# A hybrid attention and state-space layer on one core: x in whole tiles without GpSimd, y's second half in two groups, the last products and stores spread over more engines

## The chip, the cores and the metric

The kernel runs on one core of one Trainium2 chip. The metric is the time of one execution in microseconds (us); less is better. TensorE (PE) multiplies matrices, VectorE (DVE) and ScalarE (ACT) work element by element, GpSimd (POOL) does so too, and SyncE (SP) issues the transfers between HBM and the on-chip memory.

## The reference, cut to what matters

```python
hn = rms_norm(x, norm_mix)
q, k, v, gate_a, u, gate_s = split(hn @ w_in)          # 2048 -> 4608 columns
y_attn = block_attention(rope(rms(q)), rope(rms(k)), v) * silu(gate_a)
y_ssm = gelu(s5_bidirectional(u))
glu = y_ssm @ w_glu + b_glu
y_ssm = glu[:, :1024] * sigmoid(glu[:, 1024:]) * silu(gate_s)
h = x + concat(y_attn, y_ssm) @ w_out
h = h + sigmoid(rms_norm(h, norm_ple) @ w_ple_gate) * (p @ w_ple_proj)
return rms_norm(h, norm_final)                          # (1, 1024, 2048)
```

There are 1024 tokens and 2048 features, all in float32. Features lie on the 128 partitions and tokens along the free side, so x is 16 tiles (k = 0 to 15) of 128 features by 1024 tokens.

## The kernel before

Each matrix product is made of three: an operand is split into a rounded part H (ScalarE: a copy, for x with the gain as scale) and the rest L = operand minus H (VectorE), and TensorE forms H·H, H·L and L·H. Weights come in tiles of 512 columns (wraw, three buffers), and their H and L (wH, wL) have four buffers each; `w_next` hands out one tile, starts the load of the tile four further on and the split of the tile two further on.

The program is written in one order, and each engine takes its own instructions in that order; semaphores make an instruction wait for its operands and for the buffers that it overwrites. SyncE's queue is in order too: a load that waits for its buffer holds up every transfer behind it. Side work runs as generators (`bg`), each of which takes one step at each `tick`, two k tiles apart.

**The first stage** (`run`, the loop over k): for every k tile, `mm_k` forms the products with two columns of w_in (tile zf, 12 matmuls of 512 tokens per k). Around it `x_dma(k + 4)` loads x, `x_split(k + 2)` makes hH (L310, ScalarE) and hL (L311, VectorE), and `x_sq(k + 1)` sums the squares for the norm: the left token half is squared (L493) and added (L495) on GpSimd, the right half squared on ScalarE (L491) and added on VectorE (L495). Weight tiles change at every fourth k. The third column of w_in (zt) follows without a gap in the program, then the other columns with the state-space scan beside them, then attention.

**The back part** (`back(hf)`) runs once for each token half hf: products with w_glu, w_out, and then 16 rounds n of 48 matmuls with w_gate and 6 with w_proj; `fin_g` closes a round with a sigmoid (ScalarE, L1133) and a square (L1149). In the first half, the second half's y is fetched after round 10 (`y_load`, eight loads into the ring of nine buffers `cyc`), passed through GELU after round 11 (L1064, eight on ScalarE), and split in the background (`y_split`). ScalarE loads another table (ACT_TABLE_LOAD) whenever it changes between sigmoid and GELU.

**The end** (`finish(1)`): `colsum` sums the squares over the partitions with eight one-column matmuls, alternately of the running sum `acc` and of the last tile's squares; `rsqrt` and `spread` follow on VectorE, `rows` (L360) spreads the result over all partitions into PSUM, ScalarE copies it to `acc` (L1166), and VectorE forms 16 products (L1169), each stored by SyncE (L1170).

Of the kernel before, what the change touches and what calls it, by code (L numbers as in the profile page):

```python
# [9 lines left out]
F32 = mybir.dt.float32  # L10
F32R = mybir.dt.float32r
I32 = mybir.dt.int32
ALU = mybir.AluOpType
# [3 lines left out]
SEQ = 1024  # L17
# [221 lines left out]
class Kernel:  # L239
# [63 lines left out]
    def split(self, H, L, src, scale=None):  # L303

        nc = self.nc
        if scale is None:
            nc.scalar.copy(H, src)  # L307
            nc.vector.tensor_tensor(L, src, H.bitcast(F32), ALU.subtract)  # L308
        else:
            nc.scalar.activation(H, src, AF.Copy, scale=scale)  # L310
            nc.vector.scalar_tensor_tensor(L, src, scale, H.bitcast(F32), ALU.mult, ALU.subtract)  # L311
# [21 lines left out]
        nc.vector.tensor_scalar(t, t, -0.5, 1.5, ALU.mult, ALU.add)  # L333
        nc.vector.tensor_tensor(out, r, t, ALU.mult)

    def colsum(self, sqs, more=None):


        pc = self.psC("cs")
        for i, sq in enumerate(sqs):  # L340
            for b in range(4):
                c, s = 4 * i + b, slice(128 * b, 128 * b + 128)
                self.nc.tensor.matmul(
                    pc[:, c : c + 1], sq[:, s], self.ones[:, 0:1], start=True, stop=more is None
                )
                if more is not None:
                    self.nc.tensor.matmul(pc[:, c : c + 1], more[i][:, s], self.ones[:, 0:1], start=False, stop=True)
        return pc[:, 0 : 4 * len(sqs)]

    def spread(self, cols):  # L350
# [112 lines left out]
    def x_dma(self, k):  # L463
        if k >= KD:
            return
        for h in range(2):
            xt = self.xp.tile([128, 512], F32, name="xraw", tag="xraw", bufs=10)
            self.nc.sync.dma_start(xt, self.i["xT"][k][:, self.half(h)])
            self.xraw.append(xt)

    def x_split(self, k):
        H = self.b4(f"hH{k}", dt=F32R)
        L = self.b4(f"hL{k}", dt=F32R)
        self.hH.append(H)
        self.hL.append(L)
        for h in range(2):
            s = self.half(h)
            self.split(H[:, s], L[:, s], self.xraw[2 * k + h], self.g_mix[:, k : k + 1])

    def x_sq(self, k):  # L480
        nc = self.nc
        for h in range(2):
            s = self.half(h)
            xt = self.xraw[2 * k + h]
            self.xraw[2 * k + h] = None
            if k == 0:
                nc.scalar.activation(self.xsq[:, s], xt, AF.Square)
                continue
            sq = self.xp.tile([128, 512], F32, name="xq", tag="xq", bufs=4)
            if h:  # L490
                nc.scalar.activation(sq, xt, AF.Square)  # L491
            else:
                nc.gpsimd.tensor_tensor(sq, xt, xt, ALU.mult)  # L493
            eng = nc.vector if h else nc.gpsimd
            eng.tensor_tensor(self.xsq[:, s], self.xsq[:, s], sq, ALU.add)  # L495

    def x_rstd(self):
        self.rstd = self.xsq
# [549 lines left out]
            if k % 2:  # L1048
                self.tick()

    def y_load(self, hf):
        raw = []
        for j in range(8):
            t = self.cyc()
            self.nc.sync.dma_start(
                t.rearrange("p (t c) -> p t c", t=4),
                self.d_y[j][4 - 4 * hf : 8 - 4 * hf].rearrange("t f c -> f t c"),
            )
            raw.append(t)
        return raw  # L1060
# [7 lines left out]
            yield  # L1068
        self.y_gelu(raw)

    def y_split(self, hf, raw, yg, pool=False):
        split = self.split_pool if pool else self.split
        for j in range(8):
            x = self.hl(f"yg{hf}_{j}")
            v = x.rearrange("p r (t c) -> p r t c", t=4)
            split(v[:, 0], v[:, 1], raw[j].rearrange("p (t c) -> p t c", t=4)[:, ::-1, :])
            yg[j] = x
            yield

    def o_load(self, hf, mix, js=range(8)):  # L1080
        for j in js:
# [46 lines left out]
    def fin_g(self, hf, n, pg, pp, ho, hp):  # L1128
        nc = self.nc
        acc = self.xsq[:, 512:1024]  # L1130
        t = self.t2k("tz")
        nc.vector.tensor_tensor(t, pg, self.xsq[:, 0:512], ALU.mult)
        nc.scalar.activation(t, t, AF.Sigmoid)  # L1133
        last = hf == 1 and n == 15
        if last:
            nc.scalar.activation(self.rk[:, 0:1], self.ones[:, 0:1], AF.Sqrt)
        nc.vector.tensor_tensor(t, pp, t, ALU.mult)
        eng = nc.vector if last else nc.gpsimd
        eng.tensor_tensor(hp, ho, t, ALU.add)
        if last:  # L1140
            self.last_sq = self.t2k("tq")
            nc.scalar.activation(self.last_sq, hp, AF.Square)
            return
        yield
        if n == 0:
            nc.scalar.activation(acc, hp, AF.Square)
        else:
            s2 = self.t2k("tq")
            nc.scalar.activation(s2, hp, AF.Square)  # L1149
            nc.gpsimd.tensor_tensor(acc, acc, s2, ALU.add)  # L1150

    def finish(self, hf, hs):
        nc = self.nc
        acc = self.xsq[:, 512:1024]
        if hf == 0:
            for _ in range(5):
                yield
        pc = self.colsum([acc], [self.last_sq] if hf == 1 else None)
        yield
        yield  # L1160
        self.rsqrt(pc, DM, self.rk[:, 0:4])
        dg = self.spread(self.rk[:, 0:4])
        for _ in range(5):
            yield
        r = self.rows(dg)
        nc.scalar.copy(acc, r)  # L1166
        for n in range(16):
            g = self.g_fin[:, n : n + 1]
            nc.vector.scalar_tensor_tensor(hs[n], hs[n], g, acc, ALU.mult, ALU.mult)  # L1169
            nc.sync.dma_start(self.out[n][:, self.half(hf)], hs[n])  # L1170
            if hf == 0:
                yield

    def p_load(self, hf, pT):
        for k in range(2):
# [7 lines left out]
    def back(self, hf, yg, mix):  # L1183
# [19 lines left out]
        for n in range(16):  # L1203
            if n % 2 == 0:
                hp = self.b4(f"h{hf}_{n}", (128, 2, 512))
            pg = self.psC("pg")
            ho = self.cyc()
            nc.sync.dma_start(ho, self.d_h[hf][n])
            if n == 0:
                self.bg(self.h_rstd())  # L1210
            self.mm_half(pg, 16, hg)
            pp = self.psC("pp")
            self.mm_half(pp, 2, pT)
            hs.append(hp[:, n % 2])
            self.bg(self.fin_g(hf, n, pg, pp, ho, hs[n]))
            if hf == 0 and n == 10:
                raw = self.y_load(1)
            if hf == 0 and n == 11:
                self.y_gelu(raw)
                self.bg(self.y_split(1, raw, nyg))  # L1220
        self.drain()
        self.bg(self.finish(hf, hs))
        return nyg, nmix
# [11 lines left out]
    def run(self):  # L1235
# [62 lines left out]
        yg, mix = {}, {}  # L1298
        for b in self.attention():
            if b == T * (NH - 1) + 2:  # L1300
                self.bg(self.y_split(0, raw, yg, True))
            elif b == NH * T + 3:
                self.bg(self.o_load(0, mix))
        for hf in range(2):
# [101 lines left out]
```

## Time and profile before

| | us |
|---|---|
| median of three runs (2195.22 to 2196.39) | 2195.66 |
| the profiled execution's own time | 2196.16 |
| its span | 2194.4 |
| TensorE busy in the span | 2129.4 |
| VectorE, ScalarE, GpSimd busy | 1384.1, 780.0, 656.0 |

The profiled execution is 1.76 us longer than its span, and 0.50 us above the median of the runs. The profile's slices (40 of 54.9 us) show TensorE at 7 tenths in the first, 6 tenths in the last and 9 or more in all between; VectorE is at 8 tenths in the first slice, GpSimd at 6. A timeline row gives the start, the length, the engine, the line, what is written and read, and in brackets how long the engine had been idle and who ended that. Matmuls overlap, so their pitch is read from their starts.

### The profile page before, as it was taken

What the parts mean: (1) busy time and instruction counts of PE and PEld (TensorE: products, weight loads), DVE (VectorE), ACT (ScalarE), POOL (GpSimd) and SP (SyncE); (2) the same over time, 40 slices, a digit from 0 to 9 for tenths busy, and PEclk for the clock granted to TensorE, in tenths of its full rate; (3) what the DMA queues carried; (4) which work ended last, traced back from release to release, by engine and by line L of the source; (5) the groups of instructions that cost most, each with busy time, mean ns of one, the idle gap of its engine ahead of it and who ended that gap; (6) DMA issues with size and microseconds to landing.
All of it is one profiled execution on the core that took longest, in us unless ns stands there. A gap on an engine that the chain in (4) does not pass through costs nothing.

```text
span 2194.4 us, 29198 instructions
## 1 busy us (share of the span) xinstructions
PE 2129.4 (97%) x10428; PEld 1777.3 (81%) x10428; DVE 1384.1 (63%) x2292; ACT 780.0 (36%) x1438; POOL 656.0 (30%) x630
## 2 busy tenths in 40 slices
PE   7999999999999999999999999999999999999996
PEld 5788878888887888887889888888887788888885
DVE  8745678787878787847999744444444644444344
ACT  5211222222222222237777633333334333333332
POOL 6152455555655554601222100111122000111120
PEclk8999999999999999999999999999999999999998
DMA  5224223323323333342121244444343644453333
GB/s 193 85 99 124 65 76 90 94 87 85 105 81 97 87 93 86 97 150 75 39 77 39 92 137 137 146 151 124 124 139 119 213 142 144 144 153 114 126 113 125
DMA packets 173313, 245.08 MB, mean 112 GB/s; under 512 B 27376, under 2 KB 77680, under 8 KB 172912
## 3 DMA queue, kind: packets, MB, share of 16 engines
q1 hardware_dynamic: 173168, 243.22, 35.6%
q8 instruction: 82, 1.34, 0.2%
q14 instruction: 63, 0.52, 0.1%
HBM read 189.35 MB, written 48.56 MB: 108 GB/s over the span
## 4 chain that ended last, share of the span: by engine, by line
PE 49%; DVE 3%; ACT 1%; DMA 1%; issue 1%; POOL 0%; DVEq 0%; SPq 0%; ACTq 0%
PE ph L1046 5%; PE ph L1047 5%; PE ph L1045 5%; PE pg L1047 5%; PE pg L1046 5%; PE pg L1045 5%; PE ptr L955 2%; PE pv L969 1%; PE pv L968 1%; PE pv L970 1%; PE S L925 1%; PE S L928 1%; PE S L924 1%; PE gg L1047 1%; PE gv L1047 1%; PE gv L1046 1%
## 5 line engine op out<-in xcount | busy, mean ns | idle before, releaser
L308 DVE TENSOR_TENSOR wL<-wraw,wH 128x512 fp32r<-128x512 f32 (+1 forms) x496 | 408.5, 844 | 451.1 <-ACT wH L307 449.5
L307 ACT CAST wH<-wraw 128x512 fp32r<-128x512 f32 (+1 forms) x496 | 294.0, 604 | 461.1 <-PE ph L1046 124.1
L1045 PE MATMUL pg<-hg,wH 128*128 128x512 f32 x512 | 200.8, 392 | 1.6 <-ACT wH L307 1.6
L1047 PE MATMUL pg<-hg,wL 128*128 128x512 f32 x512 | 199.9, 390 | 0.7 <-DVE wL L308 0.7
L1046 PE MATMUL pg<-hg,wH 128*128 128x512 f32 x512 | 199.7, 390 | 0.0
L1113 POOL TENSOR_TENSOR xsq<-xsq,tz 128x512 f32<-128x512 f32 x30 | 39.0, 1301 | 517.8 <-ACT tz L1112 517.8
L837 ACT COPY ks<-kp 16x224 f32<-16x224 f32 x32 | 10.8, 336 | 340.3 <-DVE ks L836 189.2
L1045 PEld LDWEIGHTS pg<-hg,wH 128*128 128x128 f32 x512 | 96.3, 188 | 22.4 <-ACT wH L307 2.0
L1047 PEld LDWEIGHTS pg<-hg,wL 128*128 128x128 f32 x512 | 96.4, 188 | 21.1 <-DVE wL L308 1.2
L1046 PEld LDWEIGHTS pg<-hg,wH 128*128 128x128 f32 x512 | 96.4, 188 | 20.5 <-issue 0.5
L519 PE MATMUL zga<-hH,wH 128*128 128x512 f32 x256 | 104.0, 406 | 0.0
L519 PE MATMUL zq<-hH,wH 128*128 128x512 f32 x256 | 103.5, 404 | 0.0
L519 PE MATMUL zgs<-hH,wH 128*128 128x512 f32 x256 | 102.6, 401 | 0.0
L520 PE MATMUL zq<-hL,wH 128*128 128x512 f32 x256 | 100.7, 394 | 0.0
L520 PE MATMUL zgs<-hL,wH 128*128 128x512 f32 x256 | 100.4, 392 | 0.0
L520 PE MATMUL zga<-hL,wH 128*128 128x512 f32 x256 | 100.2, 391 | 0.0
L1045 PE MATMUL ph<-ma,wH 128*128 128x512 f32 x256 | 99.6, 389 | 0.0
L1046 PE MATMUL ph<-ma,wH 128*128 128x512 f32 x256 | 99.6, 389 | 0.0
L1047 PE MATMUL ph<-ma,wL 128*128 128x512 f32 x256 | 99.6, 389 | 0.0
L1045 PE MATMUL ph<-ms,wH 128*128 128x512 f32 x256 | 99.6, 389 | 0.0
L1046 PE MATMUL ph<-ms,wH 128*128 128x512 f32 x256 | 99.6, 389 | 0.0
L1047 PE MATMUL ph<-ms,wL 128*128 128x512 f32 x256 | 99.6, 389 | 0.0
(420 smaller groups left out, 5432.6 us busy)
## 6 DMA issues: line engine op xcount, KB each, us to landing
wraw<-in_w_in_dram SPq DMA_DIRECT2D x144, 256.0 KB
wraw<-in_w_out_dram SPq DMA_DIRECT2D x128, 256.0 KB
wraw<-in_w_gate_dram SPq DMA_DIRECT2D x128, 256.0 KB
wraw<-in_w_glu_dram SPq DMA_DIRECT2D x64, 256.0 KB
xraw<-in_xT_dram SPq DMA_DIRECT2D x32, 256.0 KB
out_dram<-h SPq DMA_DIRECT2D x32, 256.0 KB
t<-zz SPq DMA_DIRECT2D x40, 128.0 KB
d_u<-tz SPq DMA_DIRECT2D x16, 256.0 KB
```

The lines of the kernel that those rows point to most:

```text
L307: nc.scalar.copy(H, src)
L308: nc.vector.tensor_tensor(L, src, H.bitcast(F32), ALU.subtract)
L519: nc.tensor.matmul(ps[h], H[:, kk, :], rH[:, s], start=(k == 0), stop=False)
L520: nc.tensor.matmul(ps[h], H[:, kk, :], rL[:, s], start=False, stop=False)
L924: nc.tensor.matmul(S[:, s], qH[:, qs], kH[:, s], start=True, stop=False)
L925: nc.tensor.matmul(S[:, s], qH[:, qs], kL[:, s], start=False, stop=False)
L928: nc.tensor.matmul(S[:, s], qL[:, qs], kH[:, s], start=False, stop=True)
L955: nc.tensor.transpose(pc[:, b], P[:, 512 * hf + 128 * b : 512 * hf + 128 * b + 128], self.ident)
L1045: nc.tensor.matmul(ps, H[:, k % 4], x[:, 0], start=(k == 0), stop=False)
L1046: nc.tensor.matmul(ps, H[:, k % 4], x[:, 1], start=False, stop=False)
L1047: nc.tensor.matmul(ps, L[:, k % 4], x[:, 0], start=False, stop=(k == nk - 1))
L1113: nc.gpsimd.tensor_tensor(acc, acc, s2, ALU.add)
```

## The change

x comes in tiles of 128 by 1024 (five buffers instead of ten halves), split and squared in one instruction each (k = 0 still in halves for load and split); GpSimd has no part in it. The second half of y is loaded one tile at a time between the weight loads, after round 10, in two groups of four, each with its own GELU and split (`y_next`). At the end, the sum of `acc` is formed by itself and kept in `part`, and the last tile's sum is added to it; every third h tile is scaled by its gain beforehand on ScalarE, and its product formed on GpSimd from the copy; VectorE's 11 products read the spread row from PSUM; and odd tiles are stored from ScalarE's queue.

```diff
 def colsum(self, sqs):
...
-        for h in range(2):
-            xt = self.xp.tile([128, 512], F32, name="xraw", tag="xraw", bufs=10)
-            self.nc.sync.dma_start(xt, self.i["xT"][k][:, self.half(h)])
-            self.xraw.append(xt)
+        xt = self.xp.tile([128, SEQ], F32, name="xraw", tag="xraw", bufs=5)
+        for s in [self.half(0), self.half(1)] if k == 0 else [slice(0, SEQ)]:
+            self.nc.sync.dma_start(xt[:, s], self.i["xT"][k][:, s])
+        self.xraw.append(xt)
...
+        for s in [self.half(0), self.half(1)] if k == 0 else [slice(0, SEQ)]:
+            self.split(H[:, s], L[:, s], self.xraw[k][:, s], self.g_mix[:, k : k + 1])
...
-            sq = self.xp.tile([128, 512], F32, name="xq", tag="xq", bufs=4)
-            if h:
-                nc.scalar.activation(sq, xt, AF.Square)
-            else:
-                nc.gpsimd.tensor_tensor(sq, xt, xt, ALU.mult)
-            eng = nc.vector if h else nc.gpsimd
-            eng.tensor_tensor(self.xsq[:, s], self.xsq[:, s], sq, ALU.add)
+        sq = self.xp.tile([128, SEQ], F32, name="xq", tag="xq", bufs=2)
+        nc.scalar.activation(sq, xt, AF.Square)
+        nc.vector.tensor_tensor(self.xsq, self.xsq, sq, ALU.add)
...
+    def y_next(self, yg):
+        for q in range(2):
+            raw = []
+            for j in range(4 * q, 4 * q + 4):
+                raw += self.y_load(1, [j])
+                yield
+                yield
+            yield
+            yield
+            self.y_gelu(raw)
+            yield from self.y_split(1, raw, yg, 4 * q)
...
+        if hf == 1 and n % 3 == 2:
+            nc.scalar.activation(hp, hp, AF.Copy, scale=self.g_fin[:, n : n + 1])
...
-        pc = self.colsum([acc], [self.last_sq] if hf == 1 else None)
+        pc = self.colsum([acc])
+        if hf == 1:
+            part = self.t2k("tq", (128, 4))
+            nc.vector.tensor_scalar(part, pc, 1.0, None, ALU.mult)
+            pc = self.colsum([self.last_sq])
+            nc.vector.tensor_tensor(part, pc, part, ALU.add)
+            pc = part
...
-            nc.vector.scalar_tensor_tensor(hs[n], hs[n], g, acc, ALU.mult, ALU.mult)
-            nc.sync.dma_start(self.out[n][:, self.half(hf)], hs[n])
+            if hf == 1 and n % 3 == 2:
+                nc.gpsimd.tensor_tensor(hs[n], hs[n], acc, ALU.mult)
+            else:
+                nc.vector.scalar_tensor_tensor(hs[n], hs[n], g, r if hf == 1 else acc, ALU.mult, ALU.mult)
             if hf == 0:
                 yield
+            eng = nc.scalar if hf == 1 and n % 2 else nc.sync
+            eng.dma_start(self.out[n][:, self.half(hf)], hs[n])
...
             if hf == 0 and n == 10:
-                raw = self.y_load(1)
-            if hf == 0 and n == 11:
-                self.y_gelu(raw)
-                self.bg(self.y_split(1, raw, nyg))
+                self.bg(self.y_next(nyg))
```

The order on VectorE at the start of the first stage, before (hL, wL, xsq as above; a row gives line, operation, what is written and read, the size):

```order
L308 TENSOR_TENSOR wL<-wraw,wH 128x512
L311 SCALAR_TENSOR_TENSOR hL_220<-xraw,vec,hH_219 128x512 x2
L308 TENSOR_TENSOR wL<-wraw,wH 128x512 x2
L311 SCALAR_TENSOR_TENSOR hL_260<-xraw,vec,hH_259 128x512 x2
L495 TENSOR_TENSOR xsq<-xsq,xq 128x512
L311 SCALAR_TENSOR_TENSOR hL_288<-xraw,vec,hH_287 128x512 x2
```

The same place after the change, from k = 1 on:

```order
L308 TENSOR_TENSOR wL<-wraw,wH 128x512
L311 SCALAR_TENSOR_TENSOR hL_213<-xraw,vec,hH_212 128x1024
L308 TENSOR_TENSOR wL<-wraw,wH 128x512 x2
L311 SCALAR_TENSOR_TENSOR hL_248<-xraw,vec,hH_247 128x1024
L483 TENSOR_TENSOR xsq<-xsq,xq 128x1024
L311 SCALAR_TENSOR_TENSOR hL_269<-xraw,vec,hH_268 128x1024
```

The sequence is the same; a pair of halves has become one instruction, and the sum of squares covers both halves on VectorE.

On ScalarE at rounds 11 and 12 of the first token half, before (yg is the split y, tz the sigmoid of a round, tq its square, wH the weights):

```order
L307 CAST wH<-wraw 128x512 x2
L1064 ACT_TABLE_LOAD
L1064 ACTIVATE z<-z 128x512
L1064 ACTIVATE W<-W 128x512 x2
L1064 ACTIVATE tab<-tab 128x512
L1064 ACTIVATE E<-E 128x512
L1064 ACTIVATE WT<-WT 128x512
L1064 ACTIVATE r_15170<-r_15170 128x512
L1064 ACTIVATE r_15172<-r_15172 128x512
L307 CAST wH<-wraw 128x512
L1133 ACT_TABLE_LOAD
L1133 ACTIVATE tz<-tz 128x512
```

After the change, the first of the two groups:

```order
L307 CAST wH<-wraw 128x512 x3
L1134 ACTIVATE tz<-tz 128x512
L1052 ACT_TABLE_LOAD
L1052 ACTIVATE W<-W 128x512 x2
L1052 ACTIVATE tab<-tab 128x512
L1052 ACTIVATE E<-E 128x512
L307 CAST yg_0_15186<-W 128x512
L1150 ACTIVATE tq<-h_10_14954 128x512
L307 CAST wH<-wraw 128x512
```

Four GELUs stand between two weight casts where eight stood, the sigmoid of round 11 is now ahead of them, and there are four table loads around y where there were two.

At the end, on VectorE after the change, with the engines that an instruction waits for (tq is `part`, bc the spread row in PSUM):

```order
L1164 TENSOR_SCALAR tq<-cs 128x4 [waits PE_49,Pool_49]
L1166 TENSOR_TENSOR tq<-cs,tq 128x4 [waits DVE_49,PE_49]
L325 TENSOR_SCALAR tq<-tq 128x4 [waits DVE_49,Activation_49]
L330 RECIPROCAL tq<-tq 128x4 [waits Activation_49]
L331 TENSOR_TENSOR tq<-tq 128x4 [waits DVE_49]
L332 TENSOR_TENSOR tq<-tq 128x4 [waits DVE_49]
L333 TENSOR_SCALAR tq<-tq 128x4 [waits DVE_49]
L334 TENSOR_TENSOR rk<-tq 128x4 [waits DVE_49]
L349 TENSOR_SCALAR tq<-ident,rk 128x128 [waits DVE_49]
L349 TENSOR_SCALAR tq<-ident,rk 128x128 x3
L1181 SCALAR_TENSOR_TENSOR h_0_17674<-h_0_17674,vec,bc 128x512 [waits Activation_49]
```

The first product reads the spread row from PSUM, and what it waits for is an instruction of ScalarE: the copy of that row, which is the last one that ScalarE computes.

## Rows read from the trace of the kernel before

**Rows 1.** Waits of TensorE, whole span: us in total, times, longest us.

```profile
PE zf L520 <- DVE hL L311: 12.6, 8, 2.9
```

**Rows 2.** Timeline of TensorE, first stage: start us, us, instruction, [idle before].

```profile
6.08 0.80 PE L519 MATMUL zf<-hH,wH 128*128 128x512 f32 x1 [6.08 <-ACT hH L310]
...
17.22 0.80 PE L520 MATMUL zf<-hL,wH 128*128 128x512 f32 x1 [2.06 <-DVE hL L311]
...
74.64 0.39 PE L519 MATMUL zt<-hH,wH 128*128 128x512 f32 x1
```

**Rows 3.** Timeline of VectorE, first stage.

```profile
13.25 2.47 DVE L308 TENSOR_TENSOR wL<-wraw,wH 128x512 fp32r<-128x512 f32 x2 [0.68 <-ACT wH L307]
...
23.17 2.19 DVE L311 SCALAR_TENSOR_TENSOR hL<-xraw,vec,hH 128x512 fp32r<-128x512 f32 x2
...
25.28 1.78 DVE L495 TENSOR_TENSOR xsq<-xsq,xq 128x512 f32<-128x512 f32 x1
```

**Rows 4.** Instructions by source line: duration ns min/median/max, first and last start.

```profile
L495 POOL TENSOR_TENSOR xsq<-xsq,xq x15: 1302/1616/1628, 10.7 to 65.3; 128x512 f32<-128x512 f32 x15
...
L495 DVE TENSOR_TENSOR xsq<-xsq,xq x15: 677/1771/1784, 18.8 to 70.7; 128x512 f32<-128x512 f32 x15
...
L311 DVE SCALAR_TENSOR_TENSOR hL<-xraw,vec,hH x32: 737/1088/1778, 6.1 to 69.3; 128x512 fp32r<-128x512 f32 x32
...
L308 DVE TENSOR_TENSOR wL<-wraw,wH x496: 409/693/1786, 5.2 to 2164.2; 128x512 fp32r<-128x512 f32 x155, 128x256 fp32r<-128x256 f32 x11
...
L539 DVE TENSOR_TENSOR tz<-zu,xsq x10: 676/682/692, 122.0 to 209.6; 128x512 f32<-128x512 f32 x10
```

**Rows 5.** Groups by form, whole span: busy us, mean ns, idle before.

```profile
L307 ACT CAST wH<-wraw 128x512 fp32r<-128x512 f32 x464 | 284.1, 618 | 458.9 <-PE ph L1046 124.1 <-DMA wraw<-in_w_gate_dram 91.0 <-PE zu L520 52.1
...
L307 ACT CAST wH<-wraw 128x256 fp32r<-128x256 f32 x32 | 12.9, 402 | 2.2 <-DMA wraw<-in_w_proj_dram 2.2
```

**Rows 6.** Stretches: PE, PEld, DVE, ACT, POOL busy us, PEclk, DMA share, GB/s.

```profile
17.20:24.10 6.90, 6.42 (x14) 4.63 (x15) 6.90 (x7) 3.79 (x7) 4.96 (x4) 0.51 0.88 321
...
120.00:140.00 20.00, 20.00 (x90) 16.57 (x89) 5.02 (x10) 2.49 (x4) 19.06 (x37) 1.00 0.22 66
```

**Rows 7.** Timeline of SyncE's queue, first stage.

```profile
20.55 11.27 SPq L393 DMA_DIRECT2D wraw<-in_w_in_dram  x2
```

**Rows 8.** Timeline of ScalarE, first stage.

```profile
35.47 1.43 ACT L310 ACTIVATE hH<-xraw,vec 128x512 fp32r<-128x512 f32 x2 [5.40 <-DMA xraw<-in_xT_dram]
```

**Rows 9.** Timeline of TensorE near the end of the first token half.

```profile
1659.69 0.39 PE L1045 MATMUL pg<-hg,wH 128*128 128x512 f32 x1
...
1661.51 0.39 PE L1047 MATMUL pg<-hg,wL 128*128 128x512 f32 x1
...
1663.46 0.50 PE L1045 MATMUL pg<-hg,wH 128*128 128x512 f32 x1 [1.57 <-ACT wH L307]
...
1670.30 0.40 PE L1045 MATMUL pg<-hg,wH 128*128 128x512 f32 x1
```

**Rows 10.** Timeline of ScalarE at the same place.

```profile
1651.17 1.28 ACT L1064 ACT_TABLE_LOAD   x1
...
1657.27 1.28 ACT L1133 ACT_TABLE_LOAD   x1
...
1662.80 0.61 ACT L307 CAST wH<-wraw 128x512 fp32r<-128x512 f32 x1
```

**Rows 11.** Timeline of all engines, end of the program.

```profile
2173.08 0.38 PE L347 MATMUL cs<-ones,tq 128*128 128x1 f32 x2 [2.15 <-ACT tq L1142]
...
2175.12 0.16 DVE L325 TENSOR_SCALAR tq<-cs 128x4 f32<-128x4 f32 x1 [2.75 <-PE cs L347]
...
2179.60 0.59 ACT L1166 COPY xsq<-bc 128x512 f32<-128x512 f32 x1 [4.08 <-PE bc L360]
...
2180.22 10.69 DVE L1169 SCALAR_TENSOR_TENSOR h<-h,vec,xsq 128x512 f32<-128x512 f32 x16 [2.79 <-ACT xsq L1166]
```

**Rows 12.** A stretch of the last stores, columns as in group 6.

```profile
2183.00:2190.50 7.50, 0.00 (x0) 0.00 (x0) 7.50 (x12) 0.00 (x0) 0.00 (x0) 0.50 1.02 393
```

More of the change, by code (lines that the diff above doesn't have):

```diff
@@ L334, in rsqrt, with colsum @@
         nc.vector.tensor_tensor(out, r, t, ALU.mult)
-    def colsum(self, sqs, more=None):
+    def colsum(self, sqs):
         pc = self.psC("cs")
@@ L342, in colsum @@
                 c, s = 4 * i + b, slice(128 * b, 128 * b + 128)
[L343 to L347, printed above, removed]
+                self.nc.tensor.matmul(pc[:, c : c + 1], sq[:, s], self.ones[:, 0:1], start=True, stop=True)
         return pc[:, 0 : 4 * len(sqs)]
@@ L475, in x_split @@
         self.hL.append(L)
-        for h in range(2):
-            s = self.half(h)
-            self.split(H[:, s], L[:, s], self.xraw[2 * k + h], self.g_mix[:, k : k + 1])
+        for s in [self.half(0), self.half(1)] if k == 0 else [slice(0, SEQ)]:
+            self.split(H[:, s], L[:, s], self.xraw[k][:, s], self.g_mix[:, k : k + 1])
     def x_sq(self, k):
         nc = self.nc
[L482 to L488, printed above, removed]
-            sq = self.xp.tile([128, 512], F32, name="xq", tag="xq", bufs=4)
-            if h:
-                nc.scalar.activation(sq, xt, AF.Square)
-            else:
-                nc.gpsimd.tensor_tensor(sq, xt, xt, ALU.mult)
-            eng = nc.vector if h else nc.gpsimd
-            eng.tensor_tensor(self.xsq[:, s], self.xsq[:, s], sq, ALU.add)
+        xt = self.xraw[k]
+        self.xraw[k] = None
+        if k == 0:
+            nc.scalar.activation(self.xsq, xt, AF.Square)
+            return
+        sq = self.xp.tile([128, SEQ], F32, name="xq", tag="xq", bufs=2)
+        nc.scalar.activation(sq, xt, AF.Square)
+        nc.vector.tensor_tensor(self.xsq, self.xsq, sq, ALU.add)
     def x_rstd(self):
@@ L1049, in mm_half, with y_load @@
                 self.tick()
-    def y_load(self, hf):
+    def y_load(self, hf, js=range(8)):
         raw = []
-        for j in range(8):
+        for j in js:
             t = self.cyc()
@@ L1069, in y_first, with y_split @@
         self.y_gelu(raw)
-    def y_split(self, hf, raw, yg, pool=False):
+    def y_split(self, hf, raw, yg, j0=0, pool=False):
         split = self.split_pool if pool else self.split
-        for j in range(8):
+        for i in range(len(raw)):
+            j = j0 + i
             x = self.hl(f"yg{hf}_{j}")
             v = x.rearrange("p r (t c) -> p r t c", t=4)
-            split(v[:, 0], v[:, 1], raw[j].rearrange("p (t c) -> p t c", t=4)[:, ::-1, :])
+            split(v[:, 0], v[:, 1], raw[i].rearrange("p (t c) -> p t c", t=4)[:, ::-1, :])
             yg[j] = x
             yield
+    def y_next(self, yg):
[9 more added lines that the diff above has]
+            yield from self.y_split(1, raw, yg, 4 * q)
     def o_load(self, hf, mix, js=range(8)):
@@ L1300, in run @@
             if b == T * (NH - 1) + 2:
-                self.bg(self.y_split(0, raw, yg, True))
+                self.bg(self.y_split(0, raw, yg, pool=True))
             elif b == NH * T + 3:
```

## The prediction, on record before the run

> **What bounds the kernel now.** The profile's share of time says TensorE: it is busy for 2129.4 of 2194.4 us. So I read the waits of TensorE first, then the timelines around each place where it stands still, and asked there which engine ends the wait. What the change touches lies in three places.
>
> The first is the stage over k. TensorE waits eight times, 12.6 us in all, for hL, which VectorE makes [rows 1]. The stage lasts from 6.08 to 74.64 us [rows 2], and 192 matmuls are done in it. A matmul at full clock takes a step of 0.2275 us ((1661.51 - 1659.69) / 8, [rows 9]), so 12 per k tile are 2.73 us and the stage needs 43.7 us at full clock; it takes 68.6. VectorE is what is slow: its two hL of one k start at 23.17, its xsq at 25.28 [rows 3]; per k it spends 2.19 + 1.78 less overlaps of 0.08 each, 3.81 us, more than the 2.73 that TensorE wants. That these are slow rows, and not their proper cost, is to be seen from their spread: the same form of hL took between 737 and 1778 ns, of xsq between 677 and 1784 [rows 4]. GpSimd adds its half of the squares in the same stretch, at 1616 ns each. Where TensorE stands still, its granted clock falls afterwards: 0.51 over the 6.9 us that follow the wait of 2.06 us [rows 2, 6], the lower of its two levels (1.2 GHz).
>
> The second place is y. Between the starts at 1661.51 and 1670.30 lie 19 steps, 4.32 us at full pace; 8.79 passed, so 4.47 are lost [rows 9], part idle (1.57 for wH), part at the low clock behind it. ScalarE did that cast only at 1662.80, after two table loads and eight GELUs [rows 10].
>
> The third is the end: from the last square (2173.08) all is a chain, through the column sums, the root and the copy to the products at 2180.22 [rows 11], and the stores behind them, which hold the DMA engines full: share 1.02, 393 GB/s [rows 12].
>
> **The first stage after the change.** GpSimd is gone from it, so VectorE's two kinds of instruction should run at their undisturbed price, in one piece of 1024. The hL of 512 took 737 ns at best; a further 512 elements cost what wL shows from 256 to 512, (693 - 409) for 256 [rows 4], so 0.57 more: 1.31 us. The xsq: 0.68 + 0.57 = 1.25. Less the overlaps: 2.40 us per k, and for four k two wL of 0.61 (0.69 less overlap), 0.31 per k: 2.71. TensorE wants 2.73. The two are level, so TensorE should hardly wait once it has started. ScalarE takes over the other half of the squares. Its casts cost 402 ns for 256 and 618 for 512 [rows 5], so 1024 is about 1.05: hH 1.05, square 1.05 and two wH in four k, 0.31: 2.4 per k, under the 2.73.
>
> Start: VectorE gets to the wL pair at 13.25 [rows 3], which was stretched to 2.47; undisturbed 1.38, then hL 1.31: 15.9 for the hL of k = 2, which in the trace came at 17.2. TensorE would still wait some 0.9 us, and I let its clock fall as it did: 14 matmuls in 6.9 us, to 22.9. Of 192, 25 were done; 153 at 0.2275 are 34.8: the stage ends at 57.7 in place of 74.64, **16.9 us less**. Bounds: if the clock does not fall, TensorE would go at VectorE's pace, 16.0 + 14 k tiles of 2.73: 54.3 (20.3 less). At the other end, late loads of x (the first rival) give 62 to 66, 9 to 13 less.
>
> The loads are the cover that could go. SyncE stood 11.27 us at a load of weights whose buffer VectorE had still to release [rows 7]; it was free at 31.82, and ScalarE had the x behind it at 35.47, 3.65 later [rows 8], 5.40 idle. This chain stays after the change: SyncE's order is the same, with one x transfer where there were two. From the end of a group of four k: wH and wL 1.9, issue 0.9, the transfer 3.65 plus 0.65 for the second half (256 KB at 393 GB/s), hH 1.15, hL 1.31: 8.9 to 9.6 us with gaps. TensorE has work for four k, 10.9 us, so I cost it at nothing, with a cover of only 1.3 us.
>
> **y.** Ahead of the critical weight cast there are now a sigmoid (.63), one table load (1.28), four GELUs (2.1: each 0.525, since 6.10 us between the two loads hold 1.28, one cast of 0.62 and eight of them [rows 10]), a cast of yg and a square (.62 each): 5.2 us; with wH and wL 6.6, some 7.3 with gaps after the round's last product of w_gate. The tile is needed 6 + 36 steps after it, 9.55 us. Slack 2.3 us; the second group has about the same. SyncE, whose load had waited for buffers behind all eight, now waits for one y at a time. So the **4.5 us** go. Two more table loads are on ScalarE, 2.6 us, off the path by that slack. Bounds: 0 to 4.5 less.
>
> The Trainium skill, "ScalarE: Activation LUTs", section "What ACT_TABLE_LOAD costs", speaks against this part: it gives a switch 1283 ns and a drain of 1380, about 2.66 us. By it the burst would be 1.4 us longer and the slack 0.9, still no wait. The trace disagrees as far as it shows: with a drain in the 6.10 us, a GELU would have 0.35 us, less than a cast of the same size.
>
> **The end.** The column sums took 2.04 us from 2173.08 to 2175.12 [rows 11], at eight matmuls, seven of them after the last square; now four stand behind it, 1.17, and one more small VectorE instruction, 0.16 for its like in the same rows, 0.2 with its gap: **0.7 less**. The first product reads PSUM and would not need ScalarE's copy (0.59), but its row in the new order waits for ScalarE, whose last computation is that copy: I count no gain. Splitting the products gains nothing as long as the stores are the limit: 4.19 MB at 393 GB/s are 10.67 us, VectorE's 16 products 10.69 [rows 11, 12]. Afterwards VectorE has 11 of some .68 (the products that read PSUM took 676 to 692 ns while GpSimd was busy in 19 of 20 us, [rows 4, 6]), 7.4 us, GpSimd five of 1.3 (its fastest sum), 6.5. The stores that ScalarE issues wait for products, and only stores are queued behind them. Both finish before the stores. If a product were slowed to the 1.09 of the hL, 11 of them are 12.0, 1.3 more than now. Bounds: 0.6 more to 3.3 less (below). The five scalings by the gain, 0.62 each on ScalarE, lie in rounds of 54 matmuls, 12.3 us, of which ScalarE fills a third to a half over the whole span (780 of 2194 us); the last of them is a round ahead of the end: nothing.
>
> **Sum.** 2196.16 - 16.9 - 4.5 - 0.7 = 2174.06; the profiled execution is 0.5 above the median of the runs, so about 2174.0. Own range: 2168 to 2179.
>
> **Rivals.**
>
> *Late loads of x.* If the transfer behind the weights lands 1.5 to 3 us later than in rows 7 and 8 (one packet stream of 512 KB beside 512 KB of weights), the chain exceeds 10.9 us by 0.2 to 3 us, three times, each with a low-clock stretch in which 14 matmuls lose about 3 us: 4 to 12 us back, 2178 to 2186. For it: the 5.40 idle, and DMA share 0.88 at 17 to 24 us. Against: the 1.3 us of cover. Chance 0.17.
>
> *y still stalls.* Four table loads and y loads between the weights; if a late y holds SyncE, weights come late and one or two stalls like the old one (4.5) return: 2178.5 to 2183. For it: SyncE's queue is in order; against: the slack of 2.3. Chance 0.10.
>
> *Two queues raise the rate of the stores.* The products would be done about 7.4 to 8.1 us after their start, and if the stores follow at that pace, 2.6 us more are saved: 2171.5. For it: VectorE's 10.69 and the stores' 10.67 are equal, so that either may be the limit; against: the share of 1.02. Chance 0.06. The Trainium skill, "DMA: Bandwidth & Descriptors", section Specifications, puts the ceiling at 435 GB/s; by that estimate the stores could take 9.64 us, one less than by the row, 2173.
>
> *The change doesn't do what it says.* VectorE's rows are slow for a cause other than GpSimd and it stays at 3.8 per k; then the first stage gains nothing and the rest 5.2: 2191. Against: the first xsq at 677 ns and the first hL at 737, the same forms. Chance 0.03.
>
> *Slower.* TensorE and VectorE are level in the first stage, and if TensorE, waiting a little for each hL, never gets back to the full clock, 167 matmuls at twice the step (0.455) last from 16 to 92 us, 17.3 later than now, and with the 5.2 of the rest: 2208. Each matmul more at the low level costs 0.2275, so the 22.1 us of gain are gone at 97 beyond the 14, 111 of the 167. For it: the clock falls after a wait of 2 us; against: it rose by 24 us in the trace with VectorE slower than it will be. Chance 0.03.
>
> **How the numbers follow.** The forecast has 0.61. 2168 to 2184 holds the store rival, y's stalls, more than half of the late loads and, bar some tails, the forecast: 0.8. A measurement of this kernel tells some 0.2%, 4.4 us, from no change: below 2191.3 is faster. Forecast, late loads, y and stores are all there, and half of the fourth: faster 0.95, same 0.02, slower 0.03.
>
> **What would show it.** Right: hL of 1024 at 1.3 us and xsq at 1.25 with no spread; zf's last matmul near 57.7; no waits of TensorE for hL after the one near 16 us; clock 1.00 from 24 us on; no gap of TensorE over 0.3 us and clock 1.00 in rounds 11 to 14; 6.4 us from the last square to the first product, where 7.14 stood; the last stores at 390 GB/s or so. Wrong: ScalarE's hH waiting for x at k = 4, 8 or 12 with TensorE's clock at 0.5 behind it; products of VectorE over 1 us; hL still at 1.1 per half.

## The result and the profile after

The changed kernel takes 2168.31 us (median of four runs, 2165.21 to 2171.12) where the kernel before takes 2196.02: a ratio of 0.9874 [0.9856, 0.9891], 27.7 us less. The forecast was 2174.0 with 2168 to 2184 around it, so the time lies at the range's lower edge. Run once more (below), the changed kernel gave 0.9896 [0.9881, 0.9911], 2173.26 beside 2195.35: 22.1 us less, which is the sum forecast, though not by the parts forecast (below). A statement on this change finer than some 5 us is not to be had from times; the profiles say more.

The profiled execution took 2165.21 us, its span is 2163.3. Waits of TensorE in the first stage, changed kernel (in total, times, longest), which answer to [rows 1]:

```profile
PE zf L507 <- ACT hH L310: 6.2, 2, 6.1
...
PE zf L508 <- DVE hL L311: 1.5, 2, 0.8
```

Eight waits for hL have become two, of 0.70 and 0.83 us. TensorE's timeline there answers to [rows 2]:

```profile
6.05 0.80 PE L507 MATMUL zf<-hH,wH 128*128 128x512 f32 x1 [6.05 <-ACT hH L310]
...
11.75 0.50 PE L508 MATMUL zf<-hL,wH 128*128 128x512 f32 x1 [0.70 <-DVE hL L311]
...
16.06 0.50 PE L508 MATMUL zf<-hL,wH 128*128 128x512 f32 x1 [0.83 <-DVE hL L311]
...
54.77 0.39 PE L507 MATMUL zt<-hH,wH 128*128 128x512 f32 x1
```

The third column starts at 54.77 in place of 74.64. Windows of the changed kernel (busy time of PE, PEld, DVE, ACT, POOL, then clock, DMA share, GB/s):

```profile
16.10:23.00 6.90, 6.90 (x30) 5.70 (x31) 6.75 (x6) 6.08 (x8) 0.00 (x0) 1.00 0.89 345
23.00:30.40 7.40, 7.40 (x34) 6.13 (x33) 7.25 (x8) 5.14 (x7) 0.00 (x0) 1.00 0.56 176
```

In the stretch that ran at 0.51 before [rows 6] the clock is 1.00 and 30 matmuls stand where 14 did. VectorE's two instructions, changed kernel (duration min, median, max in ns; first and last start):

```profile
L311 DVE SCALAR_TENSOR_TENSOR hL<-xraw,vec,hH x17: 745/1280/1287, 6.0 to 50.4; 128x1024 fp32r<-128x1024 f32 x15, 128x512 fp32r<-128x512 f32 x2
...
L483 DVE TENSOR_TENSOR xsq<-xsq,xq x15: 1217/1218/1225, 15.9 to 52.9; 128x1024 f32<-128x1024 f32 x15
```

They have lost their spread (hL's 745 ns is that of k = 0, still in halves). At y, ScalarE's timeline, which answers to [rows 10]:

```profile
1629.59 0.63 ACT L1134 ACTIVATE tz<-tz 128x512 f32<-128x512 f32 x1 [1.36 <-DVE tz L1133]
1630.24 1.28 ACT L1052 ACT_TABLE_LOAD   x1
1631.54 1.15 ACT L1052 ACTIVATE W<-W 128x512 f32<-128x512 f32 x2
...
1634.15 0.63 ACT L1150 ACTIVATE tq<-h 128x512 f32<-128x512 f32 x1
1634.68 0.61 ACT L307 CAST wH<-wraw 128x512 fp32r<-128x512 f32 x1
```

From the sigmoid's start to the critical weight cast pass 5.1 us, and rounds 1 to 12 all take 12.24 us from the start of one to that of the next, the pace at full clock; round 12 had taken 16.72 before. Rounds 13 and 14 take 12.37 and 13.14, where both had taken 12.24 or 12.25: 1.0 us is lost again behind the second group. There the sigmoid starts 4.0 us after the round's start (0.6 in rounds without y): its table load and VectorE's product are ahead of it, the square then waits for GpSimd's sum, and the weight casts stand behind both; ScalarE's timeline, TensorE's, and the window over them:

```profile
1655.58 1.28 ACT L1134 ACT_TABLE_LOAD   x1
1657.33 0.63 ACT L1134 ACTIVATE tz<-tz 128x512 f32<-128x512 f32 x1 [0.46 <-DVE tz L1133]
1660.09 0.63 ACT L1150 ACTIVATE tq<-h 128x512 f32<-128x512 f32 x1 [2.13 <-POOL h L1140]
1660.63 1.43 ACT L307 CAST wH<-wraw 128x512 fp32r<-128x512 f32 x3
```

```profile
1662.69 0.50 PE L1035 MATMUL pg<-hg,wL 128*128 128x512 f32 x1 [0.56 <-DVE wL L308]
```

```profile
1650.00:1670.00 20.00, 19.44 (x86) 15.73 (x85) 10.25 (x16) 11.27 (x20) 2.59 (x2) 1.00 0.46 142
```

The clock does not fall behind it. The end, which answers to [rows 11]:

```profile
2142.71 0.63 ACT L1143 ACTIVATE tq<-h 128x512 f32<-128x512 f32 x1
2143.39 1.05 PE L342 MATMUL cs<-ones,tq 128*128 128x1 f32 x8 [1.48 <-ACT tq L1143]
2144.48 0.16 DVE L1166 TENSOR_TENSOR tq<-cs,tq 128x4 f32<-128x4 f32 x1 [1.73 <-PE cs L342]
...
2149.36 0.59 ACT L1175 COPY xsq<-bc 128x512 f32<-128x512 f32 x1 [4.14 <-PE bc L355]
2149.97 7.33 DVE L1181 SCALAR_TENSOR_TENSOR h<-h,vec,bc 128x512 f32<-128x512 f32 x11 [2.84 <-ACT xsq L1175]
2150.02 6.18 POOL L1179 TENSOR_TENSOR h<-h,xsq 128x512 f32<-128x512 f32 x5 [15.93 <-ACT xsq L1175]
```

From the last square's end to the first product there are 6.63 us; VectorE's first product still waits for the copy.

Where the two profiles part is read by setting the starts of the same matmuls side by side (changed minus before, each row a stretch of the program):

```
to the third column             -19.9
third column to attention        -5.5
attention                        +0.5
attention's end to round 15      -3.5
round 15 to the spread row       -2.0
from there to the end            -0.7
sum (span 2194.4 to 2163.3)     -31.1
```

The fourth row is -4.5 up to round 13, less the 1.0 behind the second group. Of the fifth, -0.6 is the shorter column sums and -1.4 lies between the two halves, a stretch that took 275.7 to 280.5 us in the fourteen profiles. The second row is one that the prediction does not have, and the granted clock is behind it. From third column to attention the clock stood at 0.50 from 300.5 to 303.9, 665.8 to 672.6, 850.1 to 853.5 and 897.9 to 901.3 us in the kernel before, and from 644.3 to 647.7 alone after. At half the clock each us loses half a us of work: 8.5 us before and 1.7 after, a difference of 6.8 where 5.5 were measured. The first of these stretches, kernel before (VectorE, TensorE, and a window over TensorE's next 3.4 us):

```profile
298.37 1.64 DVE L308 TENSOR_TENSOR wL<-wraw,wH 128x512 fp32r<-128x512 f32 x1
300.06 0.84 PE L522 MATMUL zga<-hH,wL 128*128 128x512 f32 x2 [3.39 <-DVE wL L308]
300.50:303.90 3.40, 3.40 (x17) 3.02 (x16) 2.43 (x2) 0.00 (x0) 3.32 (x3) 0.50 0.39 155
```

and the same place after, where TensorE stood half as long and the clock stayed:

```profile
278.47 0.73 PE L510 MATMUL zga<-hH,wL 128*128 128x512 f32 x2 [1.66 <-DVE wL L308]
278.90:282.30 3.40, 3.40 (x24) 2.83 (x23) 2.65 (x2) 0.00 (x0) 3.32 (x3) 1.00 0.46 172
```

### The profile page after: what moved, and what is told of

Read it like the earlier page. It is cut to its first block, busy times and chain, and to the rows that moved or that the text cites. A ratio compares the mean times of both kernels' runs of the same rounds, so it can differ in the third digit from the quotient of the medians.

```text
span 2163.3 us, 29094 instructions
## 1 busy us (share of the span) xinstructions
PE 2112.9 (98%) x10428; PEld 1765.6 (82%) x10428; DVE 1358.0 (63%) x2274; ACT 787.9 (36%) x1429; POOL 618.1 (29%) x605
## 4 chain that ended last, share of the span: by engine, by line
PE 50%; DVE 3%; ACT 1%; issue 1%; DMA 1%; POOL 0%; DVEq 0%; SPq 0%; ACTq 0%
PE ph L1035 5%; PE ph L1033 5%; PE ph L1034 5%; PE pg L1035 5%; PE pg L1033 5%; PE pg L1034 5%; PE ptr L943 2%; PE pv L956 1%; PE pv L957 1%; PE pv L958 1%; PE S L913 1%; PE gg L1035 1%; PE S L916 1%; PE S L912 1%; PE gg L1033 1%; PE gg L1034 1%
## 5 line engine op out<-in xcount | busy, mean ns | idle before, releaser
L308 DVE TENSOR_TENSOR wL<-wraw,wH 128x512 fp32r<-128x512 f32 (+1 forms) x496 | 402.6, 832 | 445.3 <-ACT wH L307 440.0
```

## The experiments

**The first stage alone, y alone, the end alone.** Each takes the lines of that part of the diff and leaves the others as before.

> The first stage's part of the change alone. My theory (VectorE was slowed by GpSimd's squares and sums, and the three parts add up): TensorE starts the third column at 54.8 us as with the whole change (before 74.6), ScalarE's burst of eight GELUs still holds TensorE for 4.5 us late in the first token half, the end is as before, and the time is that of the whole change and 5 to 6 us more, 2172 to 2176. Rival: the parts do not add (what the first stage gains is partly taken back in the scan stage when the rest is missing): the scan stage's shift against before is not the 5 us that the changed kernel's profile shows, and the time is 2176 to 2180.

> The y part alone. My theory: nothing moves before the eleventh round of the first half, so every stage up to there starts as before within 0.3 us, the idle wait of TensorE for wH (1.57) is gone and the time is 4.5 us less than before, about 2191.5. Rival (four table loads and y loads between the weights make new waits): gain under 2 us. Second rival for the 5 us that the scan stage gained in the changed kernel: if they come from the y part's other order of buffers, they show here; if they come from the first stage, they do not.

> The end's part alone. My theory: 0.6 us from the shorter column sums and 0.8 from first product to end, as in the changed kernel's profile: about 2194.6. Rival: the 0.8 is another thing and goes: 2195.4.

Measured: the first stage alone 2174.56 us, ratio 0.9889 [0.9872, 0.9905]; y alone 2195.81, 0.999 [0.9979, 1.0]; the end alone 2193.1, 0.9981 [0.9968, 0.9994], beside 2197.5 for the kernel before (17 runs, 2191.21 to 2202.53). The first is as expected in its time; its third column starts at 56.07, 1.3 us later than expected, and the stall at y is still there. TensorE's waits for pg late in the first half, with the first stage alone:

```profile
PE pg L1038 <- ACT wH L307: 1.7, 1, 1.7
PE pg L1040 <- DVE wL L308: 0.7, 1, 0.7
```

and with y alone:

```profile
PE pg L1047 <- DVE wL L308: 0.6, 1, 0.6
```

The wait for wH goes with the y part and with it alone. The round with the stall took 16.72 us before, 15.27, 15.36 and 16.57 in the three other kernels that kept the old y (the first stage alone, the end alone, and the halves without GpSimd below); so it costs 3.0 to 4.5 us from execution to execution. In the times y's gain hardly shows (1.7 us, the interval 0 to 4.6), and the profiled execution of y alone was even 8.3 us longer than that of before. Side by side the rows show it: y alone was already 9.3 us behind when the rounds began, up to where the two kernels are the same, still 9.3 when round 12 began and 4.8 when round 13 began, 4.5 us gained as forecast; then it lost 1.0 in rounds 13 and 14 and 2.6 further on.

The end alone is 4.4 us faster by the times (1.3 to 7.0), more than the 1.4 expected, and its profile has none of that at the end: 7.44 us from the last square to the first product where the kernel before had 7.19, and 14.21 to the end where it had 14.16. TensorE's clock was at 0.50 there from the column sums on:

```profile
2169.31 1.86 PE L342 MATMUL cs<-ones,tq 128*128 128x1 f32 x8 [1.48 <-ACT tq L1137]
```

against 1.05 us at 1.00 in the changed kernel. With the clock down that early, the old end took 8.09 to the first product (the first stage alone), the changed one 7.40 to 7.45 in three profiles; so the shorter sums are worth some 0.6 us at either clock.

Both expectations on where the 5.5 us of the scan stage come from fall too: y alone has nothing of them, and the first stage alone took as long from the third column to attention (918.9 us) as the kernel before (917.7).

**Is it GpSimd, or the width of the tiles?** Two kernels, crosswise. The kernel before, in its halves of 512, without GpSimd:

```diff
-            if h:
-                nc.scalar.activation(sq, xt, AF.Square)
-            else:
-                nc.gpsimd.tensor_tensor(sq, xt, xt, ALU.mult)
-            eng = nc.vector if h else nc.gpsimd
-            eng.tensor_tensor(self.xsq[:, s], self.xsq[:, s], sq, ALU.add)
+            nc.scalar.activation(sq, xt, AF.Square)
+            nc.vector.tensor_tensor(self.xsq[:, s], self.xsq[:, s], sq, ALU.add)
```

> The kernel before with one edit: GpSimd's squares go to ScalarE and its sums to VectorE, all in the old halves of 512, with the old loads. My theory (GpSimd slowed VectorE): hL falls from 1.09 to 0.74 us and xsq from 1.77 to 0.68, VectorE's cycle per k is 4 x 0.63 + 0.31 = 2.9 against TensorE's 2.73, and the third column starts at 56 to 59 us. Rival (the width of the tiles, with half as many instructions and waits, did it): VectorE stays above 3.5 us per k and the third column starts after 68 us.

And the changed kernel, in its tiles of 1024, with GpSimd's half back:

```diff
-        nc.scalar.activation(sq, xt, AF.Square)
-        nc.vector.tensor_tensor(self.xsq, self.xsq, sq, ALU.add)
+        l, r = self.half(0), self.half(1)
+        nc.gpsimd.tensor_tensor(sq[:, l], xt[:, l], xt[:, l], ALU.mult)
+        nc.scalar.activation(sq[:, r], xt[:, r], AF.Square)
+        nc.gpsimd.tensor_tensor(self.xsq[:, l], self.xsq[:, l], sq[:, l], ALU.add)
+        nc.vector.tensor_tensor(self.xsq[:, r], self.xsq[:, r], sq[:, r], ALU.add)
```

> The changed kernel, with tiles of 1024 as changed, but the left half of the squares and of their sum back on GpSimd. My theory (GpSimd is what slowed VectorE): hL of 1024 rises from 1.28 to about 2.2 us, the half xsq to 1.7, and the third column starts at 70 to 76 us. Rival (the width did it): it starts before 60 us, since VectorE has a sum of only 512 to do.

VectorE's hL and the start of the third column, halves without GpSimd:

```profile
L311 DVE SCALAR_TENSOR_TENSOR hL<-xraw,vec,hH x32: 734/743/754, 6.2 to 51.3; 128x512 fp32r<-128x512 f32 x32
...
54.47 0.39 PE L515 MATMUL zt<-hH,wH 128*128 128x512 f32 x1
```

and tiles of 1024 with GpSimd:

```profile
L311 DVE SCALAR_TENSOR_TENSOR hL<-xraw,vec,hH x17: 750/2278/2321, 6.2 to 65.8; 128x1024 fp32r<-128x1024 f32 x15, 128x512 fp32r<-128x512 f32 x2
...
73.43 0.39 PE L510 MATMUL zt<-hH,wH 128*128 128x512 f32 x1
```

The width does nothing that shows (54.47 in halves, 54.77 in tiles of 1024), and GpSimd makes the difference: with it the stage is back at 73.43. The times agree: 2176.49, 0.99 [0.9885, 0.9915] without it; 2190.21, 0.9976 [0.9964, 0.9987] with it. Halves were better than the expected 56 to 59; TensorE did not wait for hL once.

**Does VectorE wait for GpSimd's results, or do they collide?** The changed kernel, with GpSimd working on a tile that nobody else touches:

```diff
+            self.dum = self.xp.tile([128, 256], F32, name="dum", tag="dum", bufs=1)
+            nc.gpsimd.memset(self.dum, 0.0)
...
+        for _ in range(4):
+            nc.gpsimd.tensor_tensor(self.dum, self.dum, self.dum, ALU.mult)
```

In a second kernel the loop is `range(12)`, with `nc.gpsimd.memset(self.dum, 0.0)` in place of the multiplication.

> The changed kernel, with four extra GpSimd multiplications per k on a tile of 128 x 256 that nothing else uses (its values go nowhere). My theory (what counts is that GpSimd reads on-chip memory while VectorE has two inputs there): hL and xsq of 1024 rise to 2 us or more, with no wait or semaphore between the engines, and the first stage ends 10 us or more later than 54.8. Rival (in the kernel before VectorE was slowed by waiting on GpSimd's results or buffers): the durations stay 1.28 and 1.22 and the stage ends at 54.8.

> As the kernel with the extra GpSimd multiplications, but with twelve memsets of the same 128 x 256 per k in their place, which read nothing. If reading is what collides, hL and xsq keep 1.28 and 1.22 us and the third column starts at 54.8; if GpSimd's mere use of the memory collides, they grow as there.

hL and xsq with the multiplications, and a stretch of VectorE's and GpSimd's timelines:

```profile
L311 DVE SCALAR_TENSOR_TENSOR hL<-xraw,vec,hH x17: 1002/1628/1631, 6.1 to 61.3; 128x1024 fp32r<-128x1024 f32 x15, 128x512 fp32r<-128x512 f32 x2
...
L485 DVE TENSOR_TENSOR xsq<-xsq,xq x15: 1449/1629/1631, 16.3 to 64.6; 128x1024 f32<-128x1024 f32 x15
...
29.23 1.63 DVE L311 SCALAR_TENSOR_TENSOR hL<-xraw,vec,hH 128x1024 fp32r<-128x1024 f32 x1
30.78 1.63 DVE L485 TENSOR_TENSOR xsq<-xsq,xq 128x1024 f32<-128x1024 f32 x1
...
29.86 7.69 POOL L487 TENSOR_TENSOR dum<-dum 128x256 f32<-128x256 f32 x5
```

and with the memsets:

```profile
L311 DVE SCALAR_TENSOR_TENSOR hL<-xraw,vec,hH x17: 747/1278/1287, 6.1 to 51.0; 128x1024 fp32r<-128x1024 f32 x15, 128x512 fp32r<-128x512 f32 x2
...
L485 DVE TENSOR_TENSOR xsq<-xsq,xq x15: 1216/1218/1225, 15.6 to 53.5; 128x1024 f32<-128x1024 f32 x15
...
L487 POOL MEMSET dum<- x180: 311/312/318, 2.2 to 68.3; 128x256 f32 x180
```

It is a collision: without a semaphore between them, each VectorE instruction becomes 0.35 to 0.41 us longer, and the third column starts at 66.82 (2185.24 us, 0.9947 [0.9929, 0.9964]). The size was expected larger (2 us or more); this GpSimd operation is half as long as those of the kernel before. And it is the reading, as far as memsets beside multiplications can tell: memsets, which kept GpSimd busy for 32 of the 38 us from 16 to 54, leave hL and xsq as they are, and the third column starts at 55.37. That kernel is nevertheless no faster (2183.8, 0.9948 [0.9931, 0.9965]), for a cause that the expectation did not see: the memsets last until 68.3, the scan's preparation is behind them in GpSimd's queue, VectorE waits 16.56 us for a load that follows from it, and TensorE 8.5 us for the spread row.

**The spread of the times.** The changed kernel again.

> The changed kernel once more, for its spread: its four times lay between 2165.2 and 2171.1, and its profile was of the lowest. My theory (GpSimd's and VectorE's work in the scan stage meet in another phase from run to run): the first stage ends at 54.8, y and the end are as in the first profile, and what differs against it lies between 200 and 1000 us. Rival (late loads of x in some executions): the first stage's end differs by the 3 to 6 us.

2173.26 us (2170.87 to 2175.1). The third column starts at 55.66, rounds 1 to 12 take 12.24 each, rounds 13 and 14 12.58 and 13.13. Of the 6.7 us by which its profile is longer than the first, 0.9 are in the first stage, 4.7 from the third column to attention (916.9 us where the first had 912.2) and 2.7 between the two halves; attention took 1.9 less. So the expectation held for the largest part only. The same stretch took 917.7, 917.3 and 924.2 in kernels with the old first stage (before, the end alone, y alone), and 914.5 to 918.9 in five others with the new one: the 5.5 us are within what this stretch does from one execution to the next. Most of that is the granted clock. It stood at 0.50 for 3.4 us of the stretch in the first profile of the changed kernel, for 13.7 in the second, 17.1 in the kernel before and 23.9 in y alone. With half of that time taken off, the stretch takes 909.1 to 913.0 us in every profile but that with the memsets, where 912.2 to 924.2 were measured. What makes TensorE stand longer there in one execution than in another is not shown by these runs.

**y in one group of eight, and the stores on one queue.**

```diff
-        for q in range(2):
-            raw = []
-            for j in range(4 * q, 4 * q + 4):
-                raw += self.y_load(1, [j])
-                yield
-                yield
-            yield
-            yield
-            self.y_gelu(raw)
-            yield from self.y_split(1, raw, yg, 4 * q)
+        raw = []
+        for j in range(8):
+            raw += self.y_load(1, [j])
+            yield
+            yield
+        yield
+        yield
+        self.y_gelu(raw)
+        yield from self.y_split(1, raw, yg)
...
-            eng = nc.scalar if hf == 1 and n % 2 else nc.sync
-            eng.dma_start(self.out[n][:, self.half(hf)], hs[n])
+            nc.sync.dma_start(self.out[n][:, self.half(hf)], hs[n])
```

> Two edits of the changed kernel at places 500 us apart. First, y is still loaded one tile at a time, but all eight GELUs stand together. My theory (the length of ScalarE's burst ahead of the critical weight cast was the cause): TensorE stops again in the round behind it and loses 2 to 4.5 us there. Rival (the loads one by one were enough): no wait over 0.3 us. Second, all stores of the second half go through one queue. By the prediction's view (the stores' rate is the limit) the end takes 13.3 us from the first product as in the changed kernel; if the second queue saved the 0.8 us, it takes 14.1 as before.

TensorE's timeline with eight GELUs together:

```profile
1656.52 0.50 PE L1033 MATMUL pg<-hg,wH 128*128 128x512 f32 x1 [3.38 <-ACT wH L307]
1657.92 0.79 PE L1035 MATMUL pg<-hg,wL 128*128 128x512 f32 x1 [0.66 <-DVE wL L308]
```

Loads one by one do not help by themselves: the stall is back, and larger than the old one (3.38 and 0.66 us idle against 1.57 and 0.74). The grouping is what counts; round 13 took 18.43 us. The stores on one queue took 13.39 us from the first product, with two queues 13.37 (one execution each): taken out by itself, the second queue costs nothing.

**All products on VectorE.** The scaling beforehand and GpSimd's branch are taken out.

> The changed kernel with all 16 last products on VectorE (reading the row in PSUM), no scaling beforehand, two queues. If the products' pace (16 x 0.67 = 10.7 us) held the stores back before, the end takes 14.0 to 14.2 us from the first product; if the second queue made the difference, 13.3.

13.57 us (one execution, 2168.68). The products then end 2.9 us before the end and not 6.0, and the end stays. So neither the queue nor the products' pace by itself is why the kernel before took 14.16 there. In the three other kernels with the old end this stretch took 13.61, 14.21 and 14.22; with the changed end alone it took 14.21, in the five other profiles that have the whole changed end 13.36 to 13.66. What decides between the two is open.

**A way round the copy.** First a second spread row:

```diff
-        nc.scalar.copy(acc, r)
+        nc.scalar.copy(acc, self.rows(dg) if hf == 1 else r)
```

> The changed kernel, with the spread row formed a second time in PSUM for ScalarE's copy, so that VectorE's first product waits for TensorE alone. My theory: the first product starts 0.6 us earlier after the last square, the stores with it, and the end is 0.6 us earlier, too little for the times to show among the spread of 6 us. Rival: the second pair of matmuls delays GpSimd's five products (by 2 us) so much that the last store comes later than now.

VectorE started 5.96 us after the last square, 0.67 sooner, but the rival held: GpSimd's first product came 2.4 us after VectorE's, and the stores behind it in both queues stood, so that the end was 14.36 us after the first product (2169.91, 0.989 [0.9869, 0.9911]). Then all products on VectorE and no copy at all, the last edit being

```diff
-        nc.scalar.copy(acc, r)
+        if hf == 0:
+            nc.scalar.copy(acc, r)
```

> The changed kernel with all 16 last products on VectorE, reading the row in PSUM, and without ScalarE's copy of that row, which nobody then needs. My theory (the copy of 0.59 us is on the path, and the stores' rate bounds what follows, whoever forms the products): the first product starts 5.9 to 6.0 us after the last square (6.6 with the copy), from there to the end 13.4 to 14.2 us as in the others, so the end comes 0.6 us sooner; the times show about 27 us less than before, within a few us of the changed kernel's. Rival (the products' pace of 0.67 us holds the stores back once they start sooner): from the first product to the end it takes over 14.2 us and nothing is gained.

VectorE's first product then waits for TensorE:

```profile
2154.07 10.62 DVE L1177 SCALAR_TENSOR_TENSOR h<-h,vec,bc 128x512 f32<-128x512 f32 x16 [2.17 <-PE bc L355]
```

5.96 us to the first product and 13.57 from there: 19.53 from the last square to the end, against 20.21 with the copy and 20.0 and 20.09 in the two profiles of the changed kernel. The time, 2169.53 (2167.67 to 2171.66), 0.9885 [0.9869, 0.99], can't be told from the changed kernel's. It has fewer instructions and is half a microsecond ahead in the profile; that it beats the changed kernel is shown by the end's rows alone, and of these by the 0.67 us to the first product: what follows it varies by more.

## Why the prediction was right

**The first stage (-16.9; measured -19.9).** The mechanism held: VectorE's rows were slow because GpSimd read beside it, and undisturbed they cost 1.28 and 1.22 us, where 1.31 and 1.25 were worked out. The step that was mis-sized is "TensorE would still wait some 0.9 us, and I let its clock fall as it did". The wait came as forecast (0.83 us, behind one of 0.70 for the hL before), but the clock stayed at 1.00; the lower bound, "if the clock does not fall ... 54.3", is what happened (54.77). The prediction's own trace had a row nearer to 0.9 than the wait of 2.06: TensorE had also stood 0.64 us at 12.62, and its clock did not fall there.

```profile
12.62 0.50 PE L520 MATMUL zf<-hL,wH 128*128 128x512 f32 x1 [0.64 <-DVE hL L311]
```

**The loads' cover** held. x came late for ScalarE by 0.8 to 2.3 us; its timeline:

```profile
18.45 1.15 ACT L310 ACTIVATE hH<-xraw,vec 128x1024 fp32r<-128x1024 f32 x1 [0.82 <-DMA xraw<-in_xT_dram]
...
29.81 1.15 ACT L310 ACTIVATE hH<-xraw,vec 128x1024 fp32r<-128x1024 f32 x1 [2.26 <-DMA xraw<-in_xT_dram]
...
40.99 1.16 ACT L310 ACTIVATE hH<-xraw,vec 128x1024 fp32r<-128x1024 f32 x1 [2.07 <-DMA xraw<-in_xT_dram]
```

and TensorE waited for none of them. The rival of late loads did not come about. (Its price was also too low by its own terms: three times 0.2 to 3 us and 3 us at the low clock are 9.6 to 18, not 4 to 12.)

**y (-4.5; measured -4.5 up to round 13 and -3.5 up to round 15).** The burst of the first group was 5.1 us to the critical cast, 5.2 forecast. What was mis-sized is "the second group has about the same" slack: there the sigmoid and the square stood ahead of the weight casts, the square waiting 2.13 us for GpSimd, and rounds 13 and 14 lost 1.0 us (1.2 in the second profile), with a wait of 0.56 us where none over 0.3 was to come. The rival that y stalls again had another way in mind, a late y that holds SyncE; that one is not seen.

**The end (-0.7; measured -0.56 to the first product).** That the copy stays on the path and that VectorE's products from PSUM are not slowed (7.33 / 11 = 0.67 us) were right. That the second queue gives nothing and that GpSimd's share gives nothing is shown for each with the other in place. Behind the first product the prediction has no gain, and both profiles of the changed kernel are 0.7 to 0.8 us shorter there than that of before; the end alone is not, so what it is stays open. The Trainium skill, "DMA: Bandwidth & Descriptors", section "Issuing engines are not separate DMA queues", says that issuing on several engines saves only the issuing time; 13.39 against 13.37 us agrees. The ceiling of 435 GB/s, which the same page of the Trainium skill gives in its section "Specifications", was not reached; the best of the windows of 3 us over the last stores shows 409 (the end alone).

**The sum.** The parts whose places are known give -19.9, -3.5 and -0.6, 24.0 us. The two measurements of the changed kernel are 27.7 and 22.1; the rest is what the scan stage and the stretch between the halves do from one execution to the next, which was not in the forecast at all. That the second measurement meets the forecast's 22.1 is luck: in its profile the first stage gave 2 us more than its term (third column at 55.66), y some 1 us less, and the spread made up the rest. (The forecast also has a slip of 0.5: 2174.06 less the 0.5 that it names are 2173.6, not 2174.0.) Behind the scan stage's spread stand waits of TensorE for a weight split on VectorE, and the granted clock after them. One such split took 1.64 us at 298 us in the trace of before, with GpSimd's tables beside it, so that the same collision is a candidate for the waits; no run here takes GpSimd away from there.

## What to carry to other kernels

When one form of instruction has a spread of two to one within a stage, look first at what another engine reads beside it: taking GpSimd's share away made VectorE do twice the sum in less time (1.22 us for 1024 where 1.77 had been for 512). Helping an engine that waits behind a shared resource is only help if the helper does not use the resource. And of work that comes in a burst on an engine in order, the length of the burst ahead of the critical instruction decides: with four GELUs in place of eight the stall of 4.5 us went, and 1.0 of it came back behind the second group.

## What the runs showed of the hardware

GpSimd and VectorE took strict turns: in a stretch of the run with extra multiplications, five GpSimd operations on 128 x 256 took 7.69 us, 1.54 each, one for each of VectorE's instructions at a pitch of 1.55 (1.63 less overlap), though GpSimd's operation alone takes 0.61 at its shortest and VectorE's 1.22 to 1.28. Memsets one after another cost VectorE nothing (1.28 and 1.22 us beside them). The Trainium skill, "SBUF — State Buffer", section "Who interferes with whom", says both: a VectorE instruction with two inputs in this memory contends with a GpSimd instruction that reads it and not with one that only writes it.
